# Transposes of the second norm's rows and of the FFN's activations, placed one by one between the matmuls of their step

## The chip, the cores and the metric

The kernel runs on one core of a Trainium2 chip. The metric is the device time of one execution in microseconds (us), as the median of several runs; lower is better.

## The reference

One decoder layer over 512 tokens of width 2048, in float32: attention (eight heads of a dilated-window kind, eight differential heads) and then a SwiGLU feed-forward block, each behind a norm and with a gated residual. What the change touches lies in the second half:

```python
x = x + gt_a * rmsnorm(mix @ w_out, g_post_attn)
h = rmsnorm(x, g_pre_ffn) * (1.0 + sc_f) + sh_f
f = (silu(h @ w_gate) * (h @ w_up)) @ w_down
x = x + gt_f * rmsnorm(f, g_post_ffn)
```

`w_gate` and `w_up` are 2048 x 5632, `w_down` is 5632 x 2048.

## The kernel before, in words

**Precision and the triple of matmuls.** Each product of two float32 matrices is done as three matmuls of a faster float32 form: both operands are split into a rounded part (hi) and a rest (lo), and hi·hi, hi·lo and lo·hi are summed in PSUM. The helper `mm_x` (line 281) issues the three; lines 282, 283 and 284 are its three matmuls. The 128x128 stationary operand is a block of the activations, the moving one a row block of 512 weights. Line 282 needs the hi part of the weights, line 283 their lo part, line 284 the hi part again with the lo part of the activations.

**Steps.** The work after the first projection is a list of 610 steps. A step uses one 128x1024 weight tile. From step 80 on (output projection, gate and up, down) a step has two halves of six matmuls: two calls of `mm_x` for each token block, so 12 matmuls in the order 282, 283, 284, 282, ... The main loop (line 1771) does for step i, in this order: events that sit ahead of the matmuls (`start_ev`, `pe_ev`), the first half of the matmuls, `do_hi(i+2)` (line 1700: ScalarE, ACT, makes the hi part of the weights for two steps later, line 1704), the second half, events behind it (`post_ev`), `do_lo(i+2)` (line 1709: VectorE, DVE, makes the lo part, line 1713), and more events (`post_end`). There are three hi buffers, so `do_hi(i+2)` can start only when step i-1 has finished with its own. Each engine does its instructions in the order in which the code writes them; semaphores between engines are the only other tie.

**Transposes.** The matmuls want activations with the contracted dimension on the partitions, so two kinds of rows are transposed on TensorE (PE), 128x128 at a time, against an identity in `cst`:

- `h2_tr` (line 1180): the rows of the second norm. 16 calls (8 for each half of the tokens), each with 4 transposes at line 1189 into one PSUM bank. They belong to steps 121 to 128 (output projection) and 152 to 159 (gate and up of the first group). Behind the step's matmuls ACT and DVE scale and split the result (`go_v`) and write it to DRAM.
- `act_tr` (line 1266): the activations silu(gate)·up of each of eleven groups of 512 columns. 22 calls, each with 8 transposes at line 1276, four into PSUM bank 6 and four into bank 7. Group 0 has its two in steps 176 and 180. Groups 1 to 10 take 28 steps each, from step 176 on; counted within a group, their calls stand in steps 27 and 31. Step 31 is step 3 of the group behind it. Behind the step's matmuls ACT copies both banks to SBUF (line 1282), and DVE later forms differences of them (`act_e`, lines 1289 to 1293).

So there are 22·8 = 176 transposes of activations and 16·4 = 64 of the norm's rows, 240 in all. All stand in `pe_ev`, ahead of the first matmul of their step.

In step 25 of a group `s_act1` (line 1355) makes the first half of the activations: ACT a sigmoid (line 1357), DVE two products (lines 1358, 1359). They stand in `post_ev`, so on DVE they are ahead of `do_lo` of that step, which makes the lo part for step 27.

Of the kernel before, what the change touches and what calls it, by code (L numbers as in the profile page):

```python
# [34 lines left out]
def body(tc, t):  # L35
    nc = tc.nc
    pe, act, dve, pool, sync = nc.tensor, nc.scalar, nc.vector, nc.gpsimd, nc.sync
# [3 lines left out]
    with ctx:  # L41
# [11 lines left out]
        def PS(b, shape=(128, 512)):  # L53
            return pp.tile(list(shape), F, tag=f"b{b}", name=f"b{b}")
# [3 lines left out]
        ident, col, colg, c_in = cst[:, 0:128], cst[:, 128:288], cst[:, 288:294], cst[:, 294:310]  # L58
# [217 lines left out]
        def mm_w(ps, whi, wlo, ahi, alo, start, stop, **kw):  # L276
            pe.matmul(ps, whi, ahi, start=start, stop=False, **kw)  # L277
            pe.matmul(ps, whi, alo, start=False, stop=False, **kw)  # L278
            pe.matmul(ps, wlo, ahi, start=False, stop=stop, **kw)  # L279

        def mm_x(ps, whi, wlo, ahi, alo, start, stop, **kw):
            pe.matmul(ps, ahi, whi, start=start, stop=False, **kw)  # L282
            pe.matmul(ps, ahi, wlo, start=False, stop=False, **kw)  # L283
            pe.matmul(ps, alo, whi, start=False, stop=stop, **kw)  # L284

        def hh(kc, sl=slice(0, 512)):
            return h_hi[kc // 4][:, kc % 4, sl], h_lo[kc // 4][:, kc % 4, sl]
# [581 lines left out]
        for jj, kp in enumerate(KP_ORDER):  # L869
            for k in range(2):  # L870
                kc = 2 * kp + k
# [184 lines left out]
        for i in range(W0 + 60):  # L1056
            mm_t = 5.13 if i < W0 else 2.57
            if todo:
                hn, k, h, qbs = todo[0]
# [21 lines left out]
            while ada_todo and i < W0 + 46 and i >= 1 and t_dve + 1.14 <= t_end + (M_ADA if i < W0 else M_ADAW) and \  # L1081
                    t_dma + 1.45 <= t_end + M_DMA and len(aux[i]) < NAUX:
                t_dma += 1.45
                n, ch, hf = ada_todo.pop(0)
# [42 lines left out]
        HF = {}  # L1127
# [52 lines left out]
        def h2_tr(hf, i, b):  # L1180

            st = {}

            def go_pe():
                st["p"] = ps = PS(b, (128, 2, 256))
                for k in range(2):
                    for tl_ in range(2):
                        kc = 2 * i + k
                        pe.transpose(ps[:, k, 128 * tl_:128 * tl_ + 128],
                                     HF["x", 2 * hf + tl_][:, 128 * kc:128 * kc + 128], ident)  # L1190

            def go_v():
                ps = st["p"]
                tmp = HF["h2t"][:, i % 4, :].rearrange("p (k c) -> p k c", k=2)
                for k in range(2):
                    kc = 2 * i + k
                    G, SH = gsh[:, 2, kc:kc + 1], gsh[:, 4, kc:kc + 1]
                    if k == 0:
                        act.activation(tmp[:, k, :], ps[:, k, :], AF.Identity, scale=G, bias=SH)
                    else:  # L1200
                        dve.tensor_scalar(tmp[:, k, :], ps[:, k, :], G, SH, op0=OP.mult, op1=OP.add)
                for k in range(2):
                    a = f"A{hf + 1}{k + 1}"
                    hi, lo = SA[a, 0][:, i, :], SA[a, 1][:, i, :]
                    act.activation(hi, tmp[:, k, :], AF.Copy)
                    dve.tensor_tensor(lo, tmp[:, k, :], hi.bitcast(F), op=OP.subtract)
                act.dma_start(h2d[i][:, 2 * hf:2 * hf + 2, :], tmp)
            return go_pe, go_v
# [20 lines left out]
        def v3(p, a):  # L1229
            return p[1].rearrange("p (a c) -> p a c", a=a)  # L1230
# [35 lines left out]
        def act_tr(g, half, src, banks):  # L1266
            st = {}

            def go_pe():
                a = v3(src(), 2)  # L1270
                for f in range(2):
                    st[f] = ps = PS(banks[f], (128, 2, 256))
                    for n in range(2):
                        for tl_ in range(2):
                            c = 128 * (2 * n + f)
                            pe.transpose(ps[:, n, 128 * tl_:128 * tl_ + 128], a[:, tl_, c:c + 128], ident)  # L1276

            def go_v():
                stage.add(src())
                p = actv[g, f"v{half}"] = stage.get()  # L1280
                for f in range(2):
                    act.activation(v3(p, 4)[:, 2 * f:2 * f + 2, :], st[f], AF.Copy)
            return go_pe, go_v
# [105 lines left out]
        for hf, at in ((0, F0 + 32), (1, F0 + 36)):  # L1389
            a, b = act_tr(0, hf, lambda hf=hf: ffn["f0", hf], (6, 7))  # L1390
# [10 lines left out]
        for g in range(1, 11):  # L1401
# [13 lines left out]
            a, b = act_tr(g, 0, lambda g=g: ffn[g, "s1"], (6, 7))  # L1415
            pe_ev[b0 + 27].append((0, a))
            post_ev[b0 + 27].append(b)
            a, b = act_tr(g, 1, lambda g=g: ffn[g, "c21"], (6, 7))
# [26 lines left out]
        def w_sums(e):  # L1445
            for g in range(1, 11):
                k = e - F1 - 28 * (g - 1)
                for j in range(4):
                    if k - j == -4:
                        pool.dma_start(rawt[g, "P", j], wgu[g, 0, j], accum_op=OP.add)  # L1450
                    elif k - j == 4:
                        dve.tensor_tensor(rawt[g, "P", j], rawt[g, "P", j], rawt[g, "B22", j], op=OP.add)
                    elif k - j == 20:
                        dve.tensor_tensor(rawt[g, "P", j], rawt[g, "P", j], rawt[g, "B21", j], op=OP.add)
                        rawp.add(rawp_of.pop((g, "B21", j)))
                    elif k - j == 10:
                        pool.dma_start(rawt[g, "R", j], wgu[g, 3, j], accum_op=OP.add)

        def w_free(e):

            p = e + 2
            if F1 <= p < D0:
                g, r = divmod(p - F1, 28)
                k, j = divmod(r, 4)
                if SLOTS[k][0] not in ("P", "Q", "m2"):
                    rawp.add(rawp_of.pop((g + 1, USE[SLOTS[k][0]], j)))
# [83 lines left out]
        def d_more():  # L1550
            rawp.add(*stage.free)
            stage.free = []
# [17 lines left out]
        for i in range(8):  # L1570
            a, b = h2_tr(0, i, 4 + i % 4)
# [16 lines left out]
        for i in range(8):  # L1588
            a, b = h2_tr(1, i, 4 + i % 4)
# [94 lines left out]
        def pump_loads():  # L1684
            while ptr[0] < len(cons) and ptr[0] < used[0] + NRAW:
                it = cons[ptr[0]]
                w = wp.tile([128, 1024], F, name="w_raw", tag="raw", bufs=NRAW)
                src = steps[it[1]]["src"] if it[0] == "w" else aux[it[1]][it[2]][0]
                sync.dma_start(w, src)
                raws[it] = w  # L1690
                ptr[0] += 1

        def take(it):
            assert cons[used[0]] == it, (cons[used[0]], it)
            used[0] += 1
            return raws.pop(it)
# [3 lines left out]
        def do_hi(i):  # L1700
            if i < NSTEP:
                raw = take(("w", i)) if steps[i]["src"] is not None else steps[i]["prov"]()
                hi = wp.tile([128, 1024], R, name="w_hi", tag="hi", bufs=3)
                act.activation(hi, raw, AF.Copy)  # L1704
                hl[i] = raw, hi
                if "prep" in steps[i]:
                    steps[i]["prep"](0)

        def do_lo(i):
            if i < NSTEP:  # L1710
                raw, hi = hl[i]
                lo = wp.tile([128, 1024], R, name="w_lo", tag="lo", bufs=3)
                dve.tensor_tensor(lo, raw, hi.bitcast(F), op=OP.subtract)  # L1713
                hl[i] = hi, lo
                if "prep" in steps[i]:
                    steps[i]["prep"](1)
                pump_loads()
# [53 lines left out]
        for i in range(NSTEP):  # L1771
            for f in start_ev[i]:
                f()
            early = W0 <= i < W0 + 16
            if early:
                do_hi(i + LA)
                do_lo(i + LA)
            for _, f in sorted(pe_ev[i], key=lambda z: z[0]):
                f()
            for f in start2_ev[i]:  # L1780
                f()
            s = steps[i]
            late = i >= NSTEP - NLAST
            if not late:
                s["mm"](*hl[i], 0)
            if not early:
                do_hi(i + LA)
            for f in mid_ev[i]:
                f()
            for f in mid_act[i]:  # L1790
                f()
            if not late:
                s["mm"](*hl.pop(i), 1)
            for f in post_ev[i]:
                f()
            for f in post_late[i] + rope1[i]:
                f()
            if not early:
                do_lo(i + LA)
            for f in rope2[i]:  # L1800
                f()
            for j, (src, f) in enumerate(aux[i]):
                f(take(("a", i, j)))
                pump_loads()
            w_free(i)
            w_sums(i)
            w_load(i)
            for f in post_end[i]:
                f()
            d_sums(i)  # L1810
            d_load(i)
            if i == D0 + 15:
                d_more()
# [115 lines left out]
```

## Time and profile before

| | |
|---|---|
| median of 3 runs | 2199.48 us (2195.65 to 2199.91) |
| the profiled execution's own time | 2196.76 us |
| its span, first to last instruction | 2195.0 us (1.8 us of its time lie around it) |
| PE busy, matmuls | 2152.4 us |
| DVE busy | 1668.9 us |
| ACT busy | 1058.3 us |
| mean granted TensorE clock | 0.993 |

In the rows of the trace, PE is the matmul part of TensorE and PEld its loads of the stationary operand, which run beside the matmuls. Names such as `w_lo<-raw,w_hi` tell what is written and read. A row of the timeline has the start in us from the span's start, the duration, the engine, the line, the operation with its operands, and a count; in square brackets stands the idle time of the engine ahead of it and what ended it. A matmul's duration is a latency: the next one starts long before it ends. So the cost of an instruction in a stream is read from the distances between starts, not from durations.

### The profile page before, as it was taken

What the parts mean: (1) busy time and instruction counts of PE and PEld (TensorE: products, weight loads), DVE (VectorE), ACT (ScalarE), POOL (GpSimd) and SP (SyncE); (2) the same over time, 40 slices, a digit from 0 to 9 for tenths busy, and PEclk for the clock granted to TensorE, in tenths of its full rate; (3) what the DMA queues carried; (4) which work ended last, traced back from release to release, by engine and by line L of the source; (5) the groups of instructions that cost most, each with busy time, mean ns of one, the idle gap of its engine ahead of it and who ended that gap; (6) DMA issues with size and microseconds to landing.
All of it is one profiled execution on the core that took longest, in us unless ns stands there. A gap on an engine that the chain in (4) does not pass through costs nothing.

```text
span 2195.0 us, 26915 instructions
## 1 busy us (share of the span) xinstructions
PE 2152.4 (98%) x9748; PEld 1757.8 (80%) x9748; DVE 1668.9 (76%) x2333; ACT 1058.3 (48%) x1541; POOL 107.1 (5%) x116
## 2 busy tenths in 40 slices
PE   7999999999999999999999999999999999999997
PEld 6888777778888888777888888888888888888886
DVE  6987877776777676776777777776777788798888
ACT  5444344444435564644555554555555544444443
POOL 0000000001001000000001001000000000000000
PEclk8999999999999999999999999999999999999999
DMA  9797534545678877897778769778877889899996
GB/s 374 295 347 228 165 119 150 176 160 166 217 230 274 294 248 252 274 294 220 222 233 268 225 205 289 213 206 262 244 222 214 278 322 401 335 387 363 345 338 266
DMA packets 161028, 566.48 MB, mean 258 GB/s; under 512 B 17504, under 2 KB 17792, under 8 KB 154496
## 3 DMA queue, kind: packets, MB, share of 16 engines
q1 hardware_dynamic: 142608, 502.09, 63.8%
q0 software_dynamic: 11520, 41.95, 10.7%
q10 hardware_dynamic: 6768, 20.73, 3.1%
q8 instruction: 77, 1.26, 0.2%
q14 instruction: 55, 0.45, 0.1%
HBM read 501.77 MB, written 54.02 MB: 253 GB/s over the span
## 4 chain that ended last, share of the span: by engine, by line
PE 88%; DVE 5%; DMA 4%; ACT 1%; issue 1%; SPq 0%; POOL 0%; POOLq 0%; ACTq 0%; DVEq 0%
PE b L283 22%; PE b L282 22%; PE b L284 22%; PE b L277 6%; PE b L279 5%; PE b L278 5%; PE b L507 2%; DVE w_lo L1713 2%; DMA a<-acts 1%; PE b L545 1%; DMA raw<-in_wgu 1%; PE b L1276 1%; PE b L500 1%; PE b L529 1%; ACT w_hi L1704 1%
## 5 line engine op out<-in xcount | busy, mean ns | idle before, releaser
L1713 DVE TENSOR_TENSOR w_lo<-raw,w_hi 128x1024 fp32r<-128x1024 f32 x232 | 282.7, 1222 | 140.9 <-ACT w_hi L1704 140.7
L1704 ACT ACTIVATE w_hi<-raw 128x1024 fp32r<-128x1024 f32 x232 | 245.6, 1060 | 291.7 <-PE b L284 216.8
L282 PE MATMUL b<-w_hi,h 128*128 128x512 f32 x864 | 343.7, 398 | 2.3 <-ACT w_hi L1704 2.0
L283 PE MATMUL b<-w_lo,h 128*128 128x512 f32 x864 | 337.9, 391 | 4.1 <-DVE w_lo L1713 4.0
L284 PE MATMUL b<-w_hi,h 128*128 128x512 f32 x864 | 337.5, 391 | 0.0
L1713 DVE TENSOR_TENSOR w_lo<-w_raw,w_hi 128x1024 fp32r<-128x1024 f32 x176 | 214.2, 1221 | 61.3 <-ACT w_hi L1704 61.1
L1704 ACT ACTIVATE w_hi<-w_raw 128x1024 fp32r<-128x1024 f32 x176 | 185.2, 1055 | 142.7 <-PE b L284 58.3
L282 PE MATMUL b<-w_hi,e 128*128 128x512 f32 x640 | 249.9, 390 | 3.2 <-ACT w_hi L1704 3.2
L283 PE MATMUL b<-w_lo,e 128*128 128x512 f32 x640 | 250.1, 391 | 1.6 <-DVE w_lo L1713 1.6
L284 PE MATMUL b<-w_hi,e 128*128 128x512 f32 x640 | 249.7, 390 | 0.0
L283 PE MATMUL b<-w_lo,a 128*128 128x512 f32 x616 | 240.0, 390 | 1.1 <-DVE w_lo L1713 1.1
L282 PE MATMUL b<-w_hi,a 128*128 128x512 f32 x616 | 240.1, 390 | 1.0 <-DMA a<-acts 1.0
L284 PE MATMUL b<-w_hi,a 128*128 128x512 f32 x616 | 239.7, 389 | 0.0
L1704 ACT ACTIVATE w_hi<-w_lent 128x1024 fp32r<-128x1024 f32 x128 | 135.7, 1061 | 165.8 <-PE b L284 125.2
L1713 DVE TENSOR_TENSOR w_lo<-w_lent,w_hi 128x1024 fp32r<-128x1024 f32 x128 | 156.3, 1223 | 76.7 <-ACT w_hi L1704 76.7
L277 PE MATMUL b<-h,w_hi 128*128 128x512 f32 x512 | 213.3, 417 | 0.0
L278 PE MATMUL b<-h,w_hi 128*128 128x512 f32 x512 | 200.8, 392 | 2.5 <-DVE h L273 2.5
L279 PE MATMUL b<-h,w_lo 128*128 128x512 f32 x512 | 201.3, 393 | 0.0
L283 PEld LDWEIGHTS b<-w_lo,h 128*128 128x128 f32 x864 | 162.8, 188 | 39.8 <-DVE w_lo L1713 6.7
L282 PEld LDWEIGHTS b<-w_hi,h 128*128 128x128 f32 x864 | 162.6, 188 | 39.6 <-issue 3.7
L284 PEld LDWEIGHTS b<-w_hi,h 128*128 128x128 f32 x864 | 162.6, 188 | 34.2
L282 PEld LDWEIGHTS b<-w_hi,e 128*128 128x128 f32 x640 | 120.5, 188 | 28.5 <-ACT w_hi L1704 3.6
(348 smaller groups left out, 3448.1 us busy)
## 6 DMA issues: line engine op xcount, KB each, us to landing
a<-acts SPq DMA_DIRECT2D x154, 512.0 KB, 5.5
raw<-in_wgu SPq DMA_DIRECT2D x127, 512.0 KB, 6.6
w_raw<-in_win SPq DMA_DIRECT2D x107, 512.0 KB, 5.0
w_raw<-in_adar SPq DMA_DIRECT2D x96, 512.0 KB, 4.5
w_lent<-in_wgu SPq DMA_DIRECT2D x73, 512.0 KB, 6.2
w_raw<-in_wout SPq DMA_DIRECT2D x64, 512.0 KB, 4.8
raw<-in_wgu POOLq DMA_DIRECT2D x56, 512.0 KB, 7.0
raw<-in_wds SPq DMA_DIRECT2D x46, 512.0 KB, 6.2
```

The source lines that it names most:

```text
L277: pe.matmul(ps, whi, ahi, start=start, stop=False, **kw)
L278: pe.matmul(ps, whi, alo, start=False, stop=False, **kw)
L279: pe.matmul(ps, wlo, ahi, start=False, stop=stop, **kw)
L282: pe.matmul(ps, ahi, whi, start=start, stop=False, **kw)
L283: pe.matmul(ps, ahi, wlo, start=False, stop=False, **kw)
L284: pe.matmul(ps, alo, whi, start=False, stop=stop, **kw)
L500: pe.matmul(sc[:, r], qk[:, i, qs], qk[:, i + 1, :N], start=True, stop=True)
L507: pe.matmul(sc[:, :N], qk[k, 2 * m, qs], qk[k, 2 * m + 1, :N], start=True, stop=True)
L529: pe.transpose(tr[:, j, :], misc["p"][:, n % 2, 128 * j:128 * j + 128], ident)
L545: pe.matmul(h["pv"][:, qb, :], d["pt"][:, o:o + 128], v[:, j, e], start=j == 0, stop=j == qb)
L1704: act.activation(hi, raw, AF.Copy)
L1713: dve.tensor_tensor(lo, raw, hi.bitcast(F), op=OP.subtract)
```

## The change

`mm_x` gets a list, `between`: after each of its three matmuls it takes the first entry of that list, if there is one, and issues it. `h2_tr` and `act_tr` put their transposes into the list in `pe_ev` and no longer issue them there. So the four transposes of a norm step follow the step's matmuls 1 to 4, and the eight of an activation step follow matmuls 1 to 8. All 240 are still issued in their old step and in their old order.

```diff
+        between = []
+
         def mm_x(ps, whi, wlo, ahi, alo, start, stop, **kw):
             pe.matmul(ps, ahi, whi, start=start, stop=False, **kw)
+            if between:
+                between.pop(0)()
             pe.matmul(ps, ahi, wlo, start=False, stop=False, **kw)
+            if between:
+                between.pop(0)()
             pe.matmul(ps, alo, whi, start=False, stop=stop, **kw)
+            if between:
+                between.pop(0)()
...
                         kc = 2 * i + k
-                        pe.transpose(ps[:, k, 128 * tl_:128 * tl_ + 128],
-                                     HF["x", 2 * hf + tl_][:, 128 * kc:128 * kc + 128], ident)
+                        between.append(lambda o=ps[:, k, 128 * tl_:128 * tl_ + 128],
+                                       i_=HF["x", 2 * hf + tl_][:, 128 * kc:128 * kc + 128]: pe.transpose(o, i_, ident))
...
                             c = 128 * (2 * n + f)
-                            pe.transpose(ps[:, n, 128 * tl_:128 * tl_ + 128], a[:, tl_, c:c + 128], ident)
+                            between.append(lambda o=ps[:, n, 128 * tl_:128 * tl_ + 128],
+                                           i_=a[:, tl_, c:c + 128]: pe.transpose(o, i_, ident))
```

The order of instructions on ACT, DVE, GpSimd (POOL) and SyncE (SP) is the same before and after; only PE's differs. Lines move by 3 to 11: the three matmuls of `mm_x` are lines 285, 288 and 291 afterwards, the transposes 1199 and 1286.

PE at step 27 of group 1 before, with what each instruction waits for (`stage` holds the activations, `b` a PSUM bank, `h` a block of the second norm's rows; the row ahead is the last matmul of step 26):

```order
L284 MATMUL b_7667<-w_hi,h_111_6999 128x512
L1276 MATMUL b_8192<-cst,stage_7304 128x128 [waits DMAHW6_49,DVE_49]
L1276 MATMUL b_8192<-cst,stage_7304 128x128 x3
L1276 MATMUL b_8197<-cst,stage_7304 128x128 x4
L282 MATMUL b_7658<-w_hi,h_110_6998 128x512 [waits Activation_49]
L283 MATMUL b_7658<-w_lo,h_110_6998 128x512 [waits DVE_49]
L284 MATMUL b_7658<-w_hi,h_111_6999 128x512
```

The same place afterwards:

```order
L291 MATMUL b_7665<-w_hi,h_111_6999 128x512
L285 MATMUL b_7650<-w_hi,h_110_6998 128x512 [waits Activation_49]
L1286 MATMUL b_8192<-cst,stage_7304 128x128 [waits DMAHW6_49,DVE_49]
L288 MATMUL b_7650<-w_lo,h_110_6998 128x512 [waits DVE_49]
L1286 MATMUL b_8192<-cst,stage_7304 128x128
L291 MATMUL b_7650<-w_hi,h_111_6999 128x512
L1286 MATMUL b_8192<-cst,stage_7304 128x128
L285 MATMUL b_7650<-w_hi,h_110_6998 128x512
L1286 MATMUL b_8192<-cst,stage_7304 128x128
L288 MATMUL b_7650<-w_lo,h_110_6998 128x512
```

The matmul that waits for DVE's lo part stood behind one matmul and eight transposes of its step; now it stands behind one matmul and one transpose.

PE at step 121, the first with rows of the second norm (`x`), before:

```order
L1189 MATMUL b_6330<-cst,x_5889 128x128
L1189 MATMUL b_6330<-cst,x_5891 128x128 [waits DVE_49]
L1189 MATMUL b_6330<-cst,x_5889 128x128
L1189 MATMUL b_6330<-cst,x_5891 128x128
L282 MATMUL b_6157<-w_hi,mixhi_5809 128x512 [waits Activation_49]
L283 MATMUL b_6157<-w_lo,mixhi_5809 128x512 [waits DVE_49]
```

and afterwards:

```order
L285 MATMUL b_6157<-w_hi,mixhi_5809 128x512 [waits Activation_49]
L1199 MATMUL b_6330<-cst,x_5889 128x128
L288 MATMUL b_6157<-w_lo,mixhi_5809 128x512 [waits DVE_49]
L1199 MATMUL b_6330<-cst,x_5891 128x128
L291 MATMUL b_6157<-w_hi,mixlo_5810 128x512
L1199 MATMUL b_6330<-cst,x_5889 128x128
L285 MATMUL b_6157<-w_hi,mixhi_5809 128x512
L1199 MATMUL b_6330<-cst,x_5891 128x128
```

Four transposes in a row have become four with a matmul on each side.

More of the change, by code (lines that the diff above doesn't have):

```diff
@@ L1793, in body @@
                 s["mm"](*hl.pop(i), 1)
+            assert not between
             for f in post_ev[i]:
```

## The prediction

> **What bounds the kernel now.** I read the page first: who is busy, and what the chain that ended last is made of.
>
> ```profile
> span 2195.0 us, 26915 instructions
> PE 2152.4 (98%) x9748; PEld 1757.8 (80%) x9748; DVE 1668.9 (76%) x2333; ACT 1058.3 (48%) x1541; POOL 107.1 (5%) x116
> PE 88%; DVE 5%; DMA 4%; ACT 1%; issue 1%; SPq 0%; POOL 0%; POOLq 0%; ACTq 0%; DVEq 0%
> ```
>
> PE is busy for 98% of the span and makes 88% of the chain. So the change can act in two ways only: by what 240 transposes cost in PE's stream, one by one or in a row, and by waits of PE that appear or go when matmuls stand earlier or later in their step. Then I read PE's timeline for the distances between starts. First a block of eight transposes, step 27 of group 1, with the first of the 24 matmuls ahead of it:
>
> ```profile
> 1046.15 0.39 PE L282 MATMUL b<-w_hi,h 128*128 128x512 f32 x1
> ...
> 1051.37 0.39 PE L284 MATMUL b<-w_hi,h 128*128 128x512 f32 x1
> 1051.60 1.03 PE L1276 MATMUL b<-cst,stage 128*128 128x128 f32 x8
> 1052.39 0.48 PE L282 MATMUL b<-w_hi,h 128*128 128x512 f32 x1
> 1052.70 0.40 PE L283 MATMUL b<-w_lo,h 128*128 128x512 f32 x1
> ```
>
> From 1046.15 to 1051.37 there are 23 distances: 5.22/23 = 0.227 us for a plain matmul. The first matmul behind transposes carries an early start (its duration is 0.48 in place of 0.39), so I measure from the matmul ahead of a block to the second matmul behind it, which is two plain distances (0.454) plus the block. Here: 1052.70 - 1051.37 = 1.33, less 0.454 = 0.876 us for eight, 0.110 each.
>
> Two blocks of four, in steps 121 and 155:
>
> ```profile
> 801.81 0.39 PE L284 MATMUL b<-w_hi,mixlo 128*128 128x512 f32 x1
> ...
> 802.72 0.39 PE L283 MATMUL b<-w_lo,mixhi 128*128 128x512 f32 x1
> ```
>
> ```profile
> 900.35 0.39 PE L284 MATMUL b<-w_hi,h 128*128 128x512 f32 x1
> 900.58 0.60 PE L1189 MATMUL b<-cst,x 128*128 128x128 f32 x4
> ...
> 901.25 0.48 PE L283 MATMUL b<-w_lo,h 128*128 128x512 f32 x1
> ```
>
> 0.91 and 0.90, less 0.454: 0.451 us for four, 0.113 each. Blocks of one exist too: the attention has, in some of its units, a single transpose between two matmuls of 512 columns (line 529):
>
> ```profile
> 303.03 0.39 PE L279 MATMUL b<-h,w_lo 128*128 128x512 f32 x1
> 303.26 0.27 PE L529 MATMUL b<-cst,misc_p 128*128 128x128 f32 x1
> 303.29 0.48 PE L277 MATMUL b<-h,w_hi 128*128 128x512 f32 x1
> 303.60 0.39 PE L278 MATMUL b<-h,w_hi 128*128 128x512 f32 x1
> ```
>
> ```profile
> 366.49 0.39 PE L284 MATMUL b<-w_hi,h 128*128 128x512 f32 x1
> 366.72 0.27 PE L529 MATMUL b<-cst,misc_p 128*128 128x128 f32 x1
> ...
> 367.07 0.39 PE L283 MATMUL b<-w_lo,h 128*128 128x512 f32 x1
> ```
>
> 0.57 and 0.58, mean 0.575, less 0.454: 0.121 us for one. So a transpose costs about 0.109 plus about 0.012 for each time that the stream changes over and back.
>
> **Term 1: the stream.** An activation block goes from 0.876 to 8·0.121 = 0.968, +0.092; a norm block from 0.451 to 4·0.121 = 0.484, +0.033. With 20 activation blocks in groups 1 to 10 and 16 norm blocks that is 1.84 + 0.53 = **+2.4 us**. The rows are rounded to 0.01 us, which leaves the single one open by some 0.005 us: +1.2 to +3.5 us. That a transpose amid matmuls on both sides costs what one between two runs of matmuls costs is not shown here; with the price in a row (0.110 each) the term would be about zero, which stays as a rival.
>
> I looked for a reason why the single price could be much lower. PE's loads around the single transpose:
>
> ```profile
> 366.50 0.14 PEld L529 LDWEIGHTS b<-cst,misc_p 128*128 128x128 f32 x1
> 366.73 0.19 PEld L282 LDWEIGHTS b<-w_hi,h 128*128 128x128 f32 x1
> ```
>
> The load for the transpose (0.14) lies under the matmul that started at 366.49, and yet 0.121 us are lost, since the load of the next matmul starts only with the transpose, at 366.73. The Trainium skill, TensorE: Matmul & The Clock Gate, Part 2, says that the next tile's weights load while a matmul runs and that 128 columns stream in about 56 ns. By that rule alone a transpose between long matmuls would cost half of one in a row and the change would gain; the trace disagrees for one transpose, at 0.121 us.
>
> **Term 2: the wait for the lo part.** In each step the second matmul (line 283) is the first to need DVE's lo part. Before, in a step with transposes, it stood behind the block; now it comes after one matmul and one transpose. In step 27 of a group the lo part is late. ACT's and DVE's timelines from step 25 on, and from group 10 the row of DVE and the block on PE:
>
> ```profile
> 1046.40 1.06 ACT L1704 ACTIVATE w_hi<-w_lent 128x1024 fp32r<-128x1024 f32 x1 [1.66 <-PE b L284]
> 1047.37 1.04 ACT L1357 ACTIVATE raw<-stage 128x1024 f32<-128x1024 f32 x1
> ```
>
> ```profile
> 1048.44 1.23 DVE L1358 TENSOR_TENSOR stage<-stage,raw 128x1024 f32<-128x1024 f32 x1 [1.70 <-ACT raw L1357]
> 1049.70 1.23 DVE L1359 TENSOR_TENSOR stage<-stage,stage 128x1024 f32<-128x1024 f32 x1
> 1050.85 1.22 DVE L1713 TENSOR_TENSOR w_lo<-w_lent,w_hi 128x1024 fp32r<-128x1024 f32 x1
> ```
>
> ```profile
> 1753.24 1.22 DVE L1713 TENSOR_TENSOR w_lo<-raw,w_hi 128x1024 fp32r<-128x1024 f32 x1
> ```
>
> ```profile
> 1753.99 1.03 PE L1276 MATMUL b<-cst,stage 128*128 128x128 f32 x8
> ```
>
> The chain starts with step 25 (ACT's hi part waits for PE), goes through the sigmoid and two products, and ends with the lo part at 1050.85 + 1.22 = 1052.07, 0.47 us into step 27 (1051.60); in group 10 at 1754.46, also 0.47 into its step. Nothing in steps 25 and 26 changes, so it ends there afterwards too. Before, line 283 came at 1052.70, 0.63 later: the block hid the chain. Now the step's first matmul starts at 1051.60, the transpose at 1051.83 and the second matmul would at 1051.86: it waits. What such a short wait costs, from a place without transposes:
>
> ```profile
> 998.06 1.22 DVE L1713 TENSOR_TENSOR w_lo<-w_lent,w_hi 128x1024 fp32r<-128x1024 f32 x1
> ```
>
> ```profile
> 999.01 0.39 PE L282 MATMUL b<-w_hi,e 128*128 128x512 f32 x1
> 999.33 0.50 PE L283 MATMUL b<-w_lo,e 128*128 128x512 f32 x1
> 999.67 0.40 PE L284 MATMUL b<-w_hi,e 128*128 128x512 f32 x1
> ```
>
> The matmul starts 0.05 after the lo part's end (998.06 + 1.22 = 999.28), and the next follows 0.34 later in place of 0.227. So in step 27: start at 1052.12, the next transpose at 1052.46; without a wait it would come 0.345 (366.72 to 367.07) after the first one, at 1052.175. Lost: 0.285 us, ten times: **+2.85 us**. If only the matmul and not its load waits, its data could flow from 1051.83 + 0.11 = 1051.94 on, and the loss is 1052.12 - 1051.94 = 0.18, +1.8; above, +3.5 by rounding. I take 2.85, since the row at 999.33 is such a wait itself.
>
> Among the norm blocks one step is as tight, 155:
>
> ```profile
> 899.96 1.22 DVE L1713 TENSOR_TENSOR w_lo<-w_raw,w_hi 128x1024 fp32r<-128x1024 f32 x1
> ```
>
> The lo part ends at 901.18, the matmul starts at 901.23, the next thing at 901.57; without the wait the second transpose would be due at 900.58 + 0.23 + 0.345 = 901.155. **+0.4 us.**
>
> **What is hidden.** The transposes end later in their step, and so do ACT's copies, and DVE's differences behind these. Step 31 of group 2, first PE, then ACT, then DVE:
>
> ```profile
> 1141.32 1.03 PE L1276 MATMUL b<-cst,stage 128*128 128x128 f32 x8
> ```
>
> ```profile
> 1142.53 1.07 ACT L1282 ACTIVATE stage<-b 128x512 f32<-128x512 f32 x2
> ```
>
> ```profile
> 1143.80 0.69 DVE L1289 TENSOR_TENSOR raw<-stage 128x512 f32<-128x512 f32 x1
> ...
> 1146.22 1.23 DVE L1713 TENSOR_TENSOR w_lo<-w_lent,w_hi 128x1024 fp32r<-128x1024 f32 x1 [1.13 <-ACT w_hi L1704]
> ```
>
> The eighth transpose would start at 1141.32 + 0.23 + 7·0.345 = 1143.97 and end 0.27 later, 1144.24; the second copy (half of 1.07) ends near 1144.8; DVE's differences move from 1143.80 to there, by 1.0. DVE idles for 1.13 behind them, so its next lo part is not late. If that cover were gone, the lo part would be late by what is missing, and it is due only two steps of 2.7 us on. The queues of SP and POOL keep their order.
>
> Group 0 (steps 176 and 180) waits for data anyway; PE idles behind it:
>
> ```profile
> 1016.18 0.50 PE L282 MATMUL b<-w_hi,e 128*128 128x512 f32 x1 [3.17 <-ACT w_hi L1704]
> ```
>
> I cost its two blocks (0.18) at nothing, since they can come out of these 3.17 us. If that cover doesn't hold, add 0.18 and a wait of about one block's length (0.876) in step 180: +1.1.
>
> **Sum**: 2.4 + 2.85 + 0.4 = +5.65 us against the profiled execution: 2196.76 + 5.65 = 2202.4. That execution is 2.7 below the median of the runs, 2199.48. I take the middle between the two, 2198.1, as the base: **2203.8 us**, 0.26% above that base. About 0.2% (4.4 us) is what a measurement of this kernel can tell from no change.
>
> **Rivals.** *The wait doesn't come or costs nothing* (the lo part earlier, or PE makes it up): term 1 and step 155 alone, +2.8, 2200.9. For it: 0.47 against 0.26 into the step is a close race. Against: the chain starts from PE's own step 25, the same in groups 1 and 10. *A transpose between matmuls costs no more than in a row*: only the waits, +3.3, 2201.4. For it: nothing in the trace has one on every second place. *Faster*: the transpose's load hides under the matmul of 512 columns and it streams at the matmul's rate, 0.227/4 = 0.057 us. Then 240 of them cost 13.7 in place of 20·0.876 + 2·0.876 + 16·0.451 = 26.5, -12.8, and with the waits (+3.3) -9.5: 2188.6. It decides when the distance from the matmul ahead of a transpose to the second one behind falls under 0.56. Against: both single blocks. This is where the skill's rule above would lead. *Much slower*: the later copies push ACT's hi parts or DVE's lo parts past their due time in steps 27 and 31; a quarter of a step (0.7 us) in each of 20 steps is +14 on top, 2218. Against: the 1.13 us of idle DVE, and the two steps between a lo part and its use.
>
> **How the numbers follow.** My case 0.55; no wait 0.18; price in a row 0.13; faster 0.07; much slower 0.07. In my case the time is over the bound unless the waits come out near 1.8 and the stream near 1.2, or the runs lie low: 0.75 of it. The two small cases fall mostly within 0.2%, with one chance in six above it. That makes slower 0.41 + 0.05 + 0.07 = 0.53, faster 0.07 and 0.01 of scatter, same 0.39. The range goes from the lowest run before plus the small cases (2195.65 + 2.8, about 2198) to the highest plus the upper bounds (2199.91 + 3.5 + 3.5 + 0.4 + 1.1 = 2208.4); the two outer cases, 0.14, stay outside.
>
> **What would show it.** Right: 0.345 from transpose to transpose amid matmuls; PE idle ahead of line 288 in step 27 of every group, ended by DVE's lo part, with the next transpose some 0.28 late; none in step 31. Wrong: transposes at under 0.33 distance from each other, no wait at line 288 in step 27, or steps behind 27 and 31 that wait for hi or lo parts.

## The result, and the profile after

The changed kernel takes 2202.75 us (median of 11 runs, 2199.69 to 2205.57), against 2195.75 us of the kernel before (11 runs, 2193.13 to 2200.35). The ratio is 1.0028, with a 95% interval of 1.0020 to 1.0036: 0.28% slower, +6.1 us (4.4 to 7.9); the two medians alone lie 7.0 us apart. Timed again later it was 2202.97 against 2197.07, ratio 1.0027 (1.0017 to 1.0036). The prediction was 2203.8 us, +5.65 over a base of 2198.1.

The page of the changed kernel, the lines that answer to those of before:

```profile
span 2198.4 us, 26915 instructions
PE 2158.0 (98%) x9748; PEld 1753.3 (80%) x9748; DVE 1669.1 (76%) x2333; ACT 1064.6 (48%) x1541; POOL 107.3 (5%) x116
PE 85%; DMA 6%; DVE 6%; ACT 2%; issue 1%; SPq 0%; POOL 0%; POOLq 0%; DVEq 0%; ACTq 0%
```

The count of instructions is the same; PE is busy for 5.6 us more (2152.4 before). The page alone would say "more work on PE", but it is not all work: a matmul's duration is a latency of 0.39 us at a distance of 0.227 us, so a short wait between two starts hides under the latency drawn for the one ahead. The starts tell it. Step 27 of group 1 on PE (line 285 is the step's first matmul, 288 the one that needs the lo part, 1286 a transpose):

```profile
1051.03 0.40 PE L285 MATMUL b<-w_hi,h 128*128 128x512 f32 x1
1051.26 0.27 PE L1286 MATMUL b<-cst,stage 128*128 128x128 f32 x1
1051.55 0.51 PE L288 MATMUL b<-w_lo,h 128*128 128x512 f32 x1
1051.89 0.27 PE L1286 MATMUL b<-cst,stage 128*128 128x128 f32 x1
1051.92 0.48 PE L291 MATMUL b<-w_hi,h 128*128 128x512 f32 x1
1052.24 0.27 PE L1286 MATMUL b<-cst,stage 128*128 128x128 f32 x1
```

and on DVE:

```profile
1049.14 1.22 DVE L1369 TENSOR_TENSOR stage<-stage,stage 128x1024 f32<-128x1024 f32 x1
1050.28 1.22 DVE L1723 TENSOR_TENSOR w_lo<-w_lent,w_hi 128x1024 fp32r<-128x1024 f32 x1
```

The lo part ends at 1050.28 + 1.22 = 1051.50, 0.47 us into the step as before, and line 288 starts 0.05 later, at 1051.55. Without a wait it would start 0.03 behind the transpose, at 1051.29, as the next one does (1051.92 behind 1051.89). From first to second transpose it is 0.63 us, from second to third 0.35: 0.28 us lost. No row shows this as idle time.

Step 31 of the same group has no wait; there the transposes cost what the stream makes them cost:

```profile
1063.19 0.39 PE L285 MATMUL b<-w_hi,h 128*128 128x512 f32 x1
1063.42 0.27 PE L1286 MATMUL b<-cst,stageb 128*128 128x128 f32 x1
1063.44 0.48 PE L288 MATMUL b<-w_lo,h 128*128 128x512 f32 x1
1063.76 0.27 PE L1286 MATMUL b<-cst,stageb 128*128 128x128 f32 x1
...
1064.11 0.27 PE L1286 MATMUL b<-cst,stageb 128*128 128x128 f32 x1
...
1066.86 0.39 PE L285 MATMUL b<-w_hi,e 128*128 128x512 f32 x1
```

0.34 to 0.35 us from transpose to transpose, 0.12 more than a plain matmul; and 3.67 us from the step's start to the next step's (1066.86). Before, the same step, from its block of eight to the next step's first matmul, took 3.61:

```profile
1063.37 1.03 PE L1276 MATMUL b<-cst,stageb 128*128 128x128 f32 x8
...
1066.98 0.39 PE L282 MATMUL b<-w_hi,e 128*128 128x512 f32 x1
```

Where the wait is booked shows in the view of waits, among PE's loads, first before, then after (us in total, times, longest):

```profile
PEld b L283 <- DVE w_lo L1713: 13.3, 15, 2.5
```

```profile
PEld b L288 <- DVE w_lo L1723: 16.6, 27, 1.4
```

Twelve more waits; the second traces of the two kernels (below) have 18 and 28. Step by step, from the starts of both traces (first instruction of a step to the first of the next):

| steps | before | after | sum of the difference |
|---|---|---|---|
| 27 of groups 1 to 10 | 3.61 us each | 3.97 to 3.99 | +3.7 |
| 31 of groups 1 to 10 | 3.61 each | 3.67 to 3.69 | +0.7 |
| 155 | 3.26 | 3.59 | +0.3 |
| the other 15 with the norm's rows | 3.18 to 3.21 | 3.21 to 3.25 | +0.5 |

That is +5.2 us. The two spans differ by 3.4 only; the rest lies in steps that wait for data, in which also executions of one program differ (below).

### The profile page after: what moved, and what is told of

Read it like the earlier page. It is cut to its first block, busy times and chain, and to the rows that moved or that the text cites. A ratio compares the mean times of both kernels' runs of the same rounds, so it can differ in the third digit from the quotient of the medians.

```text
span 2198.4 us, 26915 instructions
## 1 busy us (share of the span) xinstructions
PE 2158.0 (98%) x9748; PEld 1753.3 (80%) x9748; DVE 1669.1 (76%) x2333; ACT 1064.6 (48%) x1541; POOL 107.3 (5%) x116
## 4 chain that ended last, share of the span: by engine, by line
PE 85%; DMA 6%; DVE 6%; ACT 2%; issue 1%; SPq 0%; POOL 0%; POOLq 0%; DVEq 0%; ACTq 0%
PE b L288 21%; PE b L285 21%; PE b L291 21%; PE b L277 6%; PE b L279 5%; PE b L278 5%; PE b L516 2%; DMA w_raw<-in_wout 2%; DVE w_lo L1723 2%; DMA a<-acts 1%; PE b L554 1%; ACT w_hi L1714 1%; PE b L538 1%; PE b L1286 1%; PE b L509 1%
## 5 line engine op out<-in xcount | busy, mean ns | idle before, releaser
L288 PE MATMUL b<-w_lo,h 128*128 128x512 f32 x864 | 345.1, 399 | 2.6 <-DVE w_lo L1723 2.2
L285 PE MATMUL b<-w_hi,h 128*128 128x512 f32 x864 | 345.8, 400 | 1.5 <-ACT w_hi L1714 1.1
L291 PE MATMUL b<-w_hi,h 128*128 128x512 f32 x864 | 343.7, 398 | 0.0
```

## The experiments

Theory: the stream's price (a transpose between two matmuls costs some 0.01 us more than one in a row) and the second matmul's wait for the lo part in steps 27 and 155. Rivals: the stream alone; the waits alone; data waits in steps 144 to 191 that the change moves.

**e1: only the activations one by one.** The norm's transposes stay ahead of their step (indices shortened to `...`).

```diff
-                        between.append(lambda o=ps[:, k, ...], i_=HF["x", 2 * hf + tl_][...]: pe.transpose(o, i_, ident))
+                        pe.transpose(ps[:, k, ...], HF["x", 2 * hf + tl_][...], ident)
```

> Only the 176 transposes of activations go one by one between matmuls; the 64 of the norm's rows stand ahead of their step as before. Theory (stream price and wait for the lo part): steps 27 of groups 1 to 10 last 3.98 us (3.61 before), steps 31 3.68 to 3.70 (3.61 before), steps 121 to 128 and 152 to 159 as before; +4.4 to +4.7 us over before in the whole. Rival (the change costs through data waits in steps 144 to 191 that move): steps 27 and 31 would not hold the sum, and the time would go with those data waits.

Measured: ratio to before 1.0022 (1.0012 to 1.0031), +4.8 us (2.6 to 6.8). Steps 27 last 3.97 to 3.98 us, steps 31 3.67 to 3.70, the norm's steps 3.18 to 3.28 as before. The activations alone carry about +4.4 of the step sums; what the norm's rows add, some 0.8, is too small for the times and shows in the step lengths alone.

**e2: every block at the end of its step.** No more changes of the stream than before, but no cover either.

```diff
             if not late:
                 s["mm"](*hl.pop(i), 1)
-            assert not between
+            while between:
+                between.pop(0)()
```

(and `mm_x` as before)

> All transposes of a step stand in one block behind its twelfth matmul: as few changes of the stream as before, but no cover for the wait of the second matmul. Theory: steps 31 last as before (3.61 us from first matmul to first matmul), steps 27 lose 0.29 + 0.11 = 0.40 us each (the second matmul starts 0.52 after the first in place of 0.23, and its load adds 0.11), 4.0 us; step 155 loses 0.5; in all +4.5 us over before. Rival (the price is the stream's alone): as before, 0.

Measured: ratio 1.0055 (1.0042 to 1.0068), +12.1 us: 2.7 times what was expected. Step 27 of group 1 on PE (line 286 needs the lo part):

```profile
1057.32 0.39 PE L285 MATMUL b<-w_hi,h 128*128 128x512 f32 x1
1057.84 0.50 PE L286 MATMUL b<-w_lo,h 128*128 128x512 f32 x1
1058.18 0.39 PE L287 MATMUL b<-w_hi,h 128*128 128x512 f32 x1
```

0.52 and 0.34 in place of 0.227 twice: 0.41 us lost, as expected, with no transpose in the stream there. From first matmul to first matmul steps 31 last 3.52 us and not the 3.61 expected, because the early start of the matmul behind the block falls into step 32. So two steps are taken together: 27 and 28 last 6.77 us in place of 6.33, 0.44 lost ten times; 31 and 32 last 6.34 and 6.33. So the wait alone costs, and 0.11 of it comes with the load of the waiting matmul, which starts only with that matmul, at 1057.84 too. Of the other 7.7 us, 0.5 had been foreseen, in step 155. That step lost 1.9 and grew to 5.17 us. ACT, DVE and PE there:

```profile
897.12 0.57 ACT L1202 ACTIVATE h2t<-b,gsh 128x256 f32<-128x256 f32 x1 [1.85 <-PE b L1193]
```

```profile
904.25 1.22 DVE L1717 TENSOR_TENSOR w_lo<-w_raw,w_hi 128x1024 fp32r<-128x1024 f32 x1
```

```profile
903.35 0.48 PE L285 MATMUL b<-w_hi,h 128*128 128x512 f32 x1
905.52 0.50 PE L286 MATMUL b<-w_lo,h 128*128 128x512 f32 x1 [1.70 <-DVE w_lo L1717]
```

ACT waits 1.85 us for the block at the end of step 152; from there its work and DVE's follow one behind the other without a longer pause, up to the lo part, which ends at 905.47, 2.1 us into step 155. Some 4.2 us more are in the steps 14 and 15 of eight of the groups 2 to 10 (0.2 to 1.6 us a group; the largest, in group 5, has 1.0 of its kind in a second trace of the kernel before as well). Between 920 and 1760 us ACT's copies out of PSUM wait longer for the writing of earlier activations to DRAM, in before and then in e2:

```profile
ACT stage L1343 <- DMA acts<-stage: 23.3, 8, 5.9
```

```profile
ACT stage L1347 <- DMA acts<-stage: 37.5, 8, 7.7
ACT stage L1286 <- PE b L1280: 33.6, 15, 2.5
```

The second row of e2 are the copies of the transposes' results, which wait for the block at the step's end. That later copies make later writes and so later stage buffers is argued from these rows; no run takes the write apart from the copy. What is left of the 12.1, about 1.6, is not accounted for. The changed kernel, whose last transpose ends 0.9 us earlier in its step than e2's, shows nothing of it in the steps 14 and 15 of groups 2 to 10, where its lengths are those of before to 0.03 us but for one step that is shorter. The rival "stream alone" (no loss in e2) falls.

**e3: the lo part first.** As changed, but DVE makes the lo part of step 25 ahead of the two products.

```diff
-            at(25).append(lambda g=g: s_act1(g))
+            post_end[b0 + 25].append(lambda g=g: s_act1(g))
```

> As the changed kernel, but the two products of the activations in step 25 stand behind the lo part of that step on DVE, so that the lo part for step 27 is ready some 2 us earlier. Theory: no wait in steps 27, which last 3.68 to 3.70 us like steps 31; what is left of the change is its stream price and step 155, +2.4 + 0.4 = +2.8 us over before. Rival (steps 27 are longer for another reason than the lo part): they stay at 3.98 us, +5.6 us.

Measured: ratio 1.0012 (1.0003 to 1.0020), +2.6 us (0.7 to 4.4). Steps 27 last 3.68 us in all ten groups, steps 31 3.69. Group 1 on DVE and on PE:

```profile
1047.17 1.22 DVE L1723 TENSOR_TENSOR w_lo<-w_lent,w_hi 128x1024 fp32r<-128x1024 f32 x1 [0.75 <-ACT w_hi L1714]
1048.31 1.22 DVE L1368 TENSOR_TENSOR stage<-stage,raw 128x1024 f32<-128x1024 f32 x1
```

```profile
1051.27 0.40 PE L285 MATMUL b<-w_hi,h 128*128 128x512 f32 x1
1051.50 0.28 PE L1286 MATMUL b<-cst,stage 128*128 128x128 f32 x1
1051.53 0.48 PE L288 MATMUL b<-w_lo,h 128*128 128x512 f32 x1
1051.85 0.27 PE L1286 MATMUL b<-cst,stage 128*128 128x128 f32 x1
```

The lo part is ready at 1048.39, 2.9 us ahead of the step, line 288 starts 0.03 behind the transpose, and the 0.3 us are gone from each step 27 while the order of PE is the changed kernel's. So the wait for the lo part is that part of the loss, and what stays is the stream's price.

**e4: the block behind the first matmul.** All transposes of a step in a row, one matmul later than before.

```diff
             pe.matmul(ps, ahi, whi, start=start, stop=False, **kw)
-            if between:
+            while between:
                 between.pop(0)()
```

(and no other place in `mm_x`)

> All transposes of a step in one block behind its first matmul: one change of the stream over and back, and the second matmul as late in its step as before. Theory: steps 27 and 31 last 3.61 us as before, the norm's steps too; 0 us against before, within 0.1%. Rival (transposes amid the matmuls of a step are dearer than ahead of them, whatever their order): +0.07 or more in steps 31.

Measured: ratio 1.0002 (0.9994 to 1.0011); steps 27 and 31 last 3.61 us, the norm's 3.18 to 3.28, as before. Step 27 of group 1 (line 288 needs the lo part):

```profile
1057.05 0.39 PE L285 MATMUL b<-w_hi,h 128*128 128x512 f32 x1
1057.28 1.03 PE L1282 MATMUL b<-cst,stage 128*128 128x128 f32 x8
1058.07 0.48 PE L288 MATMUL b<-w_lo,h 128*128 128x512 f32 x1
```

The second matmul comes 1.02 us into the step, behind the lo part's 0.47. A block amid the matmuls costs what one ahead of them costs, and its eight transposes again hide the lo part's delay.

**d_row and d_one: the stream's price, enlarged.** 800 transposes of the identity into free banks, in steps 6 to 15 of groups 1 to 10, in a row and one by one.

```diff
+        def extra(b):
+            ps = PS(b, (128, 4, 128))
+            for j in range(4):
+                pe.transpose(ps[:, j, :], ident, ident)
+        for g in range(1, 11):
+            for k in range(6, 16):
+                pe_ev[F1 + 28 * (g - 1) + k].append((0, lambda: (extra(6), extra(7))))
```

(d_row; in d_one `extra` appends its transposes to `between`)

> The changed kernel with 800 more transposes, of the identity into free banks: eight in a row ahead of each of the steps 6 to 15 of groups 1 to 10. They take part in no result. Theory: 0.876 to 0.885 us for each of the 100 blocks, +88 us over the changed kernel.

> The same 800 further transposes, one by one behind matmuls 1 to 8 of those steps. Theory (a transpose amid matmuls costs 0.119 to 0.121 us on every second place too): 0.95 to 0.97 us per step, +95 to +97 us over the changed kernel, so 7 to 9 us more than with the rows of eight. Rival (no dearer than in a row): +88, no difference. Rival (the load hides under the matmul and 128 columns stream in 0.057 us): +46, some 42 us less.

Measured: d_row 2284.11 us (ratio 1.0390, 1.0373 to 1.0408), d_one 2290.19 us (1.0421, 1.0405 to 1.0436): 6.1 us between them, a little under the 7 to 9 expected. Over the changed kernel that is some 80 and 87 us, under the 88 and 95 to 97 expected. Step 186 in d_row and in d_one, from its start to the start of the next:

```profile
1001.93 1.04 PE L1438 MATMUL b<-cst 128*128 128x128 f32 x8
...
1005.55 0.27 PE L1438 MATMUL b<-cst 128*128 128x128 f32 x1
```

```profile
1002.19 0.40 PE L285 MATMUL b<-w_hi,e 128*128 128x512 f32 x1
...
1005.87 0.40 PE L285 MATMUL b<-w_hi,e 128*128 128x512 f32 x1
```

3.62 and 3.68 us, which are the medians of these steps too, against 2.72 without: 0.90 and 0.96 us a step, 0.1125 us for a transpose in a row, 0.120 for one between matmuls. So on every second place it costs what the single ones in the trace of before showed (0.121), and neither rival holds: not "no dearer than in a row", and by no means the 42 us less that a load hidden under the long matmul and a stream of 0.057 us would have given. The two statements of the Trainium skill that lead there (TensorE: Matmul & The Clock Gate, Part 2: the next tile's weights load while a matmul runs, and 128 columns stream in about 56 ns) do not give the time of these transposes, 0.120 us each. The spans of the traces grew by 83.6 and 90.1 over the changed kernel, some 6 less than the price of 100 steps: steps 190 and 191, which last 6.14 and 5.94 us in the changed kernel because they wait for data, last 3.62 and 3.68 here, so their waits took that part up.

**l_after and l_before: a later lo part.** Three additions on DVE ahead of the lo part of step 25, in the changed kernel and in that of before.

```diff
+            def slow():
+                for _ in range(3):
+                    dve.tensor_tensor(junk, ident, ident, op=OP.add)
+            at(25).append(slow)
```

> The changed kernel with three small additions of 128x128 on DVE ahead of the lo part in step 25 of groups 1 to 10; they take part in no result. By the rows of 128x256 they take some 0.2 us each, an estimate. Theory: the lo part for step 27 ends about 0.6 us later, and so does the step: 4.5 to 4.6 us in place of 3.98, +6 us over the changed kernel in all.

> The kernel before with the same three additions ahead of the lo part in step 25. Theory: the block of eight ahead of the step covers 0.58 us of delay (lo part at 0.47 in the step, second matmul at 1.10, 0.05 between them), so steps 27 stay at 3.61 to 3.75 us, 0 to +1.4 us in all. Rival (steps 27 don't hang on the lo part): the additions do the same in both kernels.

Measured: l_after 1.0058 (1.0043 to 1.0073), steps 27 at 4.82 to 4.84 us; l_before 1.0017 (1.0006 to 1.0027), steps 27 at 3.99 to 4.01. Both are above what was expected (4.5 to 4.6, and 3.61 to 3.75): my estimate of the additions was too small. In l_before, DVE and then PE at step 27 of group 1:

```profile
1053.90 0.94 DVE L1414 TENSOR_TENSOR junk<-cst 128x128 f32<-128x128 f32 x3
1054.76 2.35 DVE L1717 TENSOR_TENSOR w_lo<-w_lent,w_hi 128x1024 fp32r<-128x1024 f32 x2
```

```profile
1054.66 1.03 PE L1276 MATMUL b<-cst,stage 128*128 128x128 f32 x8
1055.45 0.48 PE L282 MATMUL b<-w_hi,h 128*128 128x512 f32 x1
1056.03 0.50 PE L283 MATMUL b<-w_lo,h 128*128 128x512 f32 x1
1056.37 0.40 PE L284 MATMUL b<-w_hi,h 128*128 128x512 f32 x1
```

They take 0.86 us from start to start. With that the two kernels answer as the theory has it: in the changed one the step grows by the whole delay (4.82 - 3.98 = 0.84), in the one before by 0.40. The block covers 0.58 (lo part at 0.47, matmul at 1.10, 0.05 between), leaves 0.86 - 0.58 = 0.28 uncovered, and the waiting matmul's load adds 0.11: 0.39. So the miss is in the size of the additions, not in the cover.

**before_again and after_again: how much is scatter.** The same two programs once more.

> The kernel before once more, for a second trace of the same program. Theory: steps 27 and 31 of groups 1 to 10 and the norm's steps repeat to 0.02 us (3.61, 3.61, 3.18 to 3.21); the waits for data in steps 80 to 111 and 160 to 191 move by 1 to 2 us from execution to execution with no change in the program. Rival (those waits belong to the program's order): they repeat as well, and their difference between the kernels is the change's.

> The changed kernel once more, for the same. Theory: steps 27 3.98 and steps 31 3.68 us, step 155 3.6; +5 to +6 us over before in time, while the waits for data in steps 80 to 111 and 160 to 191 differ from those of its first trace. Rival: they repeat.

Measured: 2198.23 us (one run) and 2202.97 us, ratio 1.0027 (1.0017 to 1.0036). Steps 27 repeat to 0.02 us (3.61; 3.96 to 3.98), steps 31 too (3.61; 3.68 to 3.70). Steps 80 to 111, in which the change moves nothing, take 101.7 and 102.7 us in the two traces of before and 103.0 and 103.3 in those of the changed kernel; l_before, the same program as before up to there, takes 103.9, and l_after, d_row and d_one, the same as the changed kernel up to there, 101.3 to 101.5. Steps 144 to 191 take 153.3 and 152.4 before and 151.5 and 151.8 after. There the granted clock plays a part beside the data: between 970.1 and 973.5 us it is 0.50 in the first trace of before, with matmuls 0.43 us apart in place of 0.227, and 1.00 all through that time in after_again. So such steps move by 1 to 2 us between executions of one program, and two spans can't show a difference of some us; the length of a step that repeats in ten groups can.

## Why the prediction was right, step by step

The steps show the mechanism that was forecast, with terms that are off by some tenths of a us. That the time came so close, 2203.8 for 2202.75, is in part luck: the base of 2198.1 was 2.35 too high for the 2195.75 measured beside it, and the 5.65 were 1.35 below the distance of the two medians, 7.0.

- **Term 1, the stream** (+2.4 predicted, 1.84 for the activations and 0.53 for the norm's rows): the steps 31 gained 0.07 us each, not 0.092, so 1.4 to 1.5 us over the 20 blocks; the norm's steps 0.03 each, about 0.5. In all +2.0. The single price, 0.121, was right (0.120 in d_one). What was off is the price in a row: I took 1.33 us from rows rounded to 0.01, where a step of 3.61 less 2.72 gives 0.89 for the block, not 0.876.
- **Term 2, the wait in steps 27** (+2.85, bounds 1.8 and 3.5): 0.37 less 0.07 is 0.30 us each, +3.0. The wait comes from the lo part (e3 takes it away, l_after lengthens it one for one), and before the block covered it (e4 keeps the cover, e2 loses it, l_before uses it up). The load waits with its matmul: 0.11 us appear on top of the lateness in e2 and l_before, so the lower bound, in which only the matmul waits, falls. The sign that I had named, PE idle ahead of line 288, did not come as a row of PE: the wait shows among its loads and in the starts. The next transpose came 0.28 late, as forecast.
- **Step 155** (+0.4): 3.59 for 3.26, of which about 0.03 is the stream: +0.3. Before, it was already longer than steps 154 and 156 (3.18), so a part of the wait was there. PE and DVE there, after:

```profile
902.06 0.27 PE L1199 MATMUL b<-cst,x 128*128 128x128 f32 x1
902.43 0.50 PE L288 MATMUL b<-w_lo,h 128*128 128x512 f32 x1
902.77 0.27 PE L1199 MATMUL b<-cst,x 128*128 128x128 f32 x1
```

```profile
901.16 1.22 DVE L1723 TENSOR_TENSOR w_lo<-w_raw,w_hi 128x1024 fp32r<-128x1024 f32 x1
```

- **What was hidden.** The later copies and differences in step 31 cost nothing, as forecast: steps 32 to 36 last 2.72 us before and after. Group 0: step 180 lost 0.81 us to the wait that I had put at 0.876, here longer than the latency that hides the others, so that it shows as idle:

```profile
980.19 0.27 PE L1286 MATMUL b<-cst,stage 128*128 128x128 f32 x1
981.04 0.50 PE L288 MATMUL b<-w_lo,e 128*128 128x512 f32 x1 [0.58 <-DVE w_lo L1723]
981.38 0.27 PE L1286 MATMUL b<-cst,stage 128*128 128x128 f32 x1
```

  Against the first trace of before it was given back in steps 184 and 186 (0.64 and 0.19 us shorter), sooner than in the idle 3.17 us that I had named; e1, e3 and after_again give the same (0.79 to 0.82 lost, 0.64 and 0.19 back). Against before_again, whose steps 180, 184 and 186 are shorter themselves (3.61, 3.01 and 2.92 us for 3.73, 3.36 and 2.95), it is 0.93 lost and 0.46 back. So it is not shown that group 0 costs nothing; 0 to 0.5 us are open.
- **The sum** was 5.65; the steps hold 5.2, and the times say 6.1 (4.4 to 7.9) and 5.9 (3.7 to 7.9). The difference lies within these intervals.
- **Open**: whether the change also shortens the data waits of steps 144 to 191. The two traces of before took 152.4 and 153.3 us there, the two of the changed kernel 151.5 and 151.8, though these hold 0.6 us more of the change's own cost; e1 and e3 took 151.4 and 151.6. But l_after, the same program as the changed kernel up to there, took 153.1 (l_before 153.7). The half clock, which comes and goes between executions, is in these times: in after_again, e1 and e3 it was granted for 3.4 us in these steps, in l_after and l_before for 10.2 us, but for 10.2 in the first trace of the changed kernel as well. Nothing here settles it.

None of the runs beats the kernel before by more than the measurement can tell. e3 gets half of the loss back, and e4 all of it.

## What to carry to other kernels

A block of small instructions ahead of a step can be the cover for a chain on another engine; before it is spread, look for what stands right behind it and how long ahead of that its input is ready (here 0.63 us, less than the 0.84 by which the change brought its user forward). A wait shorter than the latency drawn for a matmul is not idle in the profile: measure it from start to start, in steps that repeat. And a price that hangs on 0.01 us times 240 is taken from a whole step's length, not from two rounded rows.

## What was not expected of the hardware

- In a stream of matmuls of 512 columns, one that waits for a semaphore costs its lateness and 0.11 us more, also when it is late by only 0.1 us: 0.34 us to the next start in place of 0.227 (999.33 to 999.67 before, 1057.84 to 1058.18 in e2, 1056.03 to 1056.37 in l_before). Amid single transposes the extra was 0.02 (1051.55 to 1051.89 in the changed kernel, against 1063.44 to 1063.76 without a wait).
- Blocks at the end of the step (e2) cost nearly three times the wait that they uncover in steps 27, +12.1 us for 4.4. In step 155 the trace shows ACT's later work as the way; in steps 14 and 15 ACT's copies waited longer, and what ties the two is not shown.
